# An MLP's second product with the activations held and 512 weight columns moved

## The chip, the cores and the metric

The kernel runs on one core of a Trainium2 chip. The time is that of the device for one execution, in microseconds (us); the median of three runs before the change is 1832.56 us (1829.42 to 1836.35).

## The reference

Two blocks in a row work on 256 tokens of 1024 channels, each with two layers. The change lies in the first block. After its attention mixers (four kinds, joined by w_out) each layer has an MLP:

```
for l in range(DEPTH):
    mod = c_act @ w_ada[l] + b_ada[l]
    sh1, sc1, g1, sh2, sc2, g2 = split(mod, 6)
    h = rmsnorm(x, norm_mix_g[l]) * (1 + sc1) + sh1
    x = x + g1 * (mixers(h @ w_in[l]) @ w_out[l])
    h = rmsnorm(x, norm_mlp_g[l]) * (1 + sc2) + sh2
    x = x + g2 * (square(relu(h @ w_up[l])) @ w_down[l])
return rmsnorm(x, final_norm_g)
```

w_up is 1024 x 4096, w_down 4096 x 1024, all in float32. The second block (a state-space scan, two attentions, gates) is the same before and after.

## The kernel before, in words

Activations lie with channels on the partitions and tokens along the free axis: x is 8 chunks of 128 channels by 256 tokens. Every large product is made of three float32r products: weight and activation are each split into a high part and the remainder (wh, wl; ah, al; uh, ul), and high x high, high x low and low x high are summed in PSUM. Weights stream from memory in tiles of 128 x 1024 (512 KB, here called half matrices) into eight buffers `w`. ScalarE copies a tile into `wh` (line 299), VectorE subtracts into `wl` (line 301); there are four buffers of each. `next_w` (line 304) asks for loads and splits ahead of their use.

The work is a queue of pieces (`add`, `fill`, `need`, lines 324 to 334). In the MLP, group g of 16 makes 256 of the 4096 hidden channels: `gemm` (line 339) runs 48 matmuls of the first product into a PSUM bank `g`, `ev_up` (line 1019) squares the positive part and splits it into uh and ul, tiles of the names pt0 and pt1. A group later `down` (line 1031) adds the second product of these 256 channels to four PSUM banks `acc` that stay for the whole MLP. In `down` the 128 x 128 weight block is held in the array and 256 tokens of uh or ul are moved past it; the result has channels on the partitions, as x has, and line 1085 adds it to x, bank by bank: two updates per bank, 128 x 256 each. The last group (`down_last`, line 1056) goes bank by bank, so that the updates of a finished bank run while the next is summed.

After layer 0 the statistics of x (`rms_wide`, line 454: squares, additions `fold`, a product `st` with ones, a power on GpSimd, a product `bc` that spreads the result) and eight half matrices each of two parts of the modulation (`ada_step`, line 551) come before the normalised chunks `ah` and `al` (`norm_apply`, line 599) and the first projections with w_in. After layer 1 the last product with the memory tokens (`tok_gemm`, line 383: it holds activations and moves 512 weight columns) runs on TensorE while the statistics are made, then the second block begins with `dt_gemm` (line 1265).

Which instruction stands where on each engine's queue is decided when the program is built, by a scheduler that simulates the engines; only the order is written into the program. Engines then run their queues strictly in order and wait on semaphores.

Of the kernel before, what the change touches and what calls it, by code (L numbers as in the profile page):

```python
# [13 lines left out]
ALU = mybir.AluOpType  # L14
PSUM = bass.MemoryType.PSUM

P = 128
S = 256
D = 1024
KC = D // P  # L20
# [473 lines left out]
def block1(e, ctx, mem0):  # L494
    nc, tc, d = e.nc, e.tc, e.d
    pool = lambda name: ctx.enter_context(tc.tile_pool(name=name, bufs=1))
    cp, zp, ap_ = pool("c1"), pool("z1"), pool("a1")
# [94 lines left out]
    def ada_add(tag, keys):  # L592
        for key in keys:
            e.add(tag, lambda key=key: (ada_pool if tag == "mlp" else ada_step)(*key[1:]))
# [26 lines left out]
    x = v3(e.unit("x"), KC)  # L621
# [368 lines left out]
    for l in range(DEPTH):  # L990
        mod = mods[l]
# [24 lines left out]
        acc = [e.bank("acc") for _ in range(4)]  # L1016
        us = {}

# [11 lines left out]

        def down(g):

            uh, ul = us[g]
            ws = {}

            def part(c, ms):
                if c not in ws:
                    ws[c] = e.next_w("w_down", l, g)
                wh, wl = ws[c]
                for m in ms:  # L1040
                    o = acc[m // 2][:, (m % 2) * S : (m % 2 + 1) * S]
                    sl = slice(m * P, (m + 1) * P)
                    fi = g == 0 and c == 0 and m % 2 == 0
                    la = g == 15 and c == 1
                    e.mm(o, wh[:, sl], uh[:, c, :], fi, False)
                    e.mm(o, wh[:, sl], ul[:, c, :], False, False)
                    e.mm(o, wl[:, sl], uh[:, c, :], False, la and m % 2 == 1)

            return part

        def down_piece(g, c):
            if c == 0:
                parts[g] = down(g)
            parts[g](c, range(KC))

        def down_last(g):
            part = down(g)
            for m in range(0, KC, 2):
                for c in range(2):
                    part(c, (m, m + 1))  # L1060

# [3 lines left out]

        parts, box, last = {}, [], {}
        steps = mlp_keys(l)
# [15 lines left out]
        ada_add("next", ad_next(l))  # L1083
        for k in range(KC):
            nc.vector.scalar_tensor_tensor(x[:, k, :], acc[k // 2][:, (k % 2) * S : (k % 2 + 1) * S], mod[:, 40 + k : 41 + k], x[:, k, :], ALU.mult, ALU.add)

# [641 lines left out]
```

## Time and profile before

| | before |
|---|---|
| median of 3 runs | 1832.56 us (1829.42 to 1836.35) |
| the profiled execution, its time | 1832.16 us |
| its span, first to last instruction | 1830.3 us |
| mean granted clock of TensorE (1 is 2.4 GHz, 0.5 is 1.2 GHz) | 0.991 |
| busy, of the span: TensorE matmuls | 98% |
| VectorE, ScalarE, GpSimd | 73%, 56%, 20% |
| chain that ended last: TensorE, VectorE, DMA, ScalarE | 89%, 4%, 3%, 3% |
| read from memory | 339 MB, 186 GB/s over the span |

Names in the profile are the program's without numbers: `acc<-pt,wh` is a matmul that writes acc and reads pt and wh. PE is TensorE, PEld its weight load, DVE is VectorE, ACT ScalarE, POOL GpSimd, SP the queue that issues the loads. A matmul's duration reaches from its start to the end of its result, and matmuls overlap; what a run of them costs is read from the start of one to the start of the next. The MLP of layer 0 lies at 216 to 404 us, that of layer 1 at 557 to 744 us.

### The profile page before, as it was taken

How to read it: one execution, taken by the hardware profiler on the slowest of the kernel's cores; microseconds unless marked ns; L12 is line 12 of the kernel's file. 1: busy time of each engine (PE TensorE's matmuls, PEld its weight loads, DVE VectorE, ACT ScalarE, POOL GpSimd, SP SyncE). 2: the span in 40 equal slices, each digit the busy share in tenths (PEclk: the TensorE clock that was granted, in tenths of full speed). 3: DMA queues.
4: the chain of work that ended last, by engine and by line, in shares of the span. 5: the costliest groups of instructions: out<-in, count | busy, mean ns of one | idle time of the engine just before them, and what ended most of it. 6: DMA issues, size and time to landing. Idle time of an engine off the chain costs nothing.

```text
span 1830.3 us, 36255 instructions
## 1 busy us (share of the span) xinstructions
PE 1789.1 (98%) x14344; PEld 1674.3 (91%) x14344; DVE 1333.6 (73%) x2209; ACT 1016.8 (56%) x1882; POOL 359.1 (20%) x291
## 2 busy tenths in 40 slices
PE   7999999999998999999999999999999999999998
PEld 6778799987888999998999999999999999999997
DVE  4575775756778655798897997576788797997566
ACT  4444444434555444567777575454556777675552
POOL 0000281800007200002444202200001444202200
PEclk9999999999998999999999999999999999999999
DMA  9873876758348655553444644465554445544451
GB/s 335 308 249 138 310 259 199 256 197 306 115 140 299 226 183 185 165 175 121 162 162 151 202 155 144 168 208 173 194 176 133 148 160 162 184 164 165 154 181 67
DMA packets 98219, 346.82 MB, mean 189 GB/s; under 512 B 12288, under 2 KB 13440, under 8 KB 97792
## 3 DMA queue, kind: packets, MB, share of 16 engines
q1 hardware_dynamic: 98048, 344.50, 55.5%
q8 instruction: 112, 1.84, 0.4%
q14 instruction: 59, 0.48, 0.1%
HBM read 339.01 MB, written 1.05 MB: 186 GB/s over the span
## 4 chain that ended last, share of the span: by engine, by line
PE 89%; DVE 4%; DMA 3%; ACT 3%; issue 1%; SPq 0%; POOLq 0%; DVEq 0%; POOL 0%; ACTq 0%
PE g L337 67%; PE acc L337 10%; PE yps L337 2%; DVE wl L301 1%; ACT wh L299 1%; PE ada L337 1%; PE o L337 1%; PE ds L337 1%; PE sc L337 1%; DMA w<-w_in 1%; PE do L337 1%; DMA w<-w_ada 1%; ACT sb L683 1%; PE xo L337 1%; DMA w<-w_up 1%
## 5 line engine op out<-in xcount | busy, mean ns | idle before, releaser
L301 DVE TENSOR_TENSOR wl<-w,wh 128x1024 fp32r<-128x1024 f32 x518 | 660.8, 1279 | 342.8 <-ACT wh L299 341.1
L299 ACT CAST wh<-w 128x1024 fp32r<-128x1024 f32 x518 | 540.5, 1047 | 494.9 <-PE g L337 328.8
L337 PE MATMUL g<-xh,wh 128*128 128x256 f32 x1664 | 478.2, 288 | 0.3
L337 PE MATMUL g<-xl,wh 128*128 128x256 f32 x1664 | 472.6, 284 | 0.0
L337 PE MATMUL g<-xh,wl 128*128 128x256 f32 x1664 | 471.8, 284 | 0.0
L337 PEld LDWEIGHTS g<-xh,wh 128*128 128x128 f32 x1664 | 319.8, 192 | 12.6 <-issue 6.2
L337 PEld LDWEIGHTS g<-xl,wh 128*128 128x128 f32 x1664 | 319.8, 192 | 0.9 <-issue 0.7
L337 PEld LDWEIGHTS g<-xh,wl 128*128 128x128 f32 x1664 | 319.9, 192 | 0.0
L337 PE MATMUL g<-ah,wh 128*128 128x256 f32 x736 | 211.5, 289 | 5.9 <-ACT ah L604 5.4
L337 PE MATMUL g<-ah,wl 128*128 128x256 f32 x736 | 210.6, 287 | 0.5 <-DVE wl L301 0.5
L337 PE MATMUL g<-al,wh 128*128 128x256 f32 x736 | 210.5, 287 | 0.5 <-DVE al L605 0.5
L403 POOL TENSOR_TENSOR rsy<-rv,mhalf 128x2 f32<-128x2 f32 (+1 forms) x14 | 14.5, 1038 | 936.8 <-DVE rv L420 830.1
L337 PE MATMUL acc<-pt,wh 128*128 128x256 f32 x1024 | 182.9, 280 | 0.0
L1505 POOL PARTITION_BROADCAST E<-rows x64 | 98.0, 1592 | 386.7 <-PE tw L1209 190.9
L1504 ACT ACTIVATE E<-E,ltok 128x128 f32<-128x128 f32 x384 | 124.3, 394 | 60.2 <-POOL E L1505 56.8
L337 PEld LDWEIGHTS acc<-pt,wh 128*128 128x128 f32 x1024 | 156.8, 188 | 0.5 <-issue 0.4
L337 PEld LDWEIGHTS g<-ah,wh 128*128 128x128 f32 x736 | 142.7, 195 | 9.8 <-ACT ah L604 6.4
L337 PEld LDWEIGHTS g<-al,wh 128*128 128x128 f32 x736 | 142.8, 194 | 2.7 <-DVE al L605 1.4
L337 PEld LDWEIGHTS g<-ah,wl 128*128 128x128 f32 x736 | 142.8, 194 | 1.2 <-DVE wl L301 0.7
L337 PE MATMUL acc<-pt,wl 128*128 128x256 f32 x512 | 142.3, 279 | 0.0
L583 POOL TENSOR_SCALAR sb<-w,ca 128x1024 f32<-128x1024 f32 x24 | 90.0, 3751 | 59.9 <-PE ada L337 32.8
L337 PEld LDWEIGHTS acc<-pt,wl 128*128 128x128 f32 x512 | 96.2, 188 | 0.0
(384 smaller groups left out, 3404.8 us busy)
## 6 DMA issues: line engine op xcount, KB each, us to landing
w<-w_ada SPq DMA_DIRECT2D x96, 512.0 KB
w<-w_up SPq DMA_DIRECT2D x64, 512.0 KB
w<-w_down SPq DMA_DIRECT2D x64, 512.0 KB
w<-w_br SPq DMA_DIRECT2D x64, 512.0 KB
w<-w_gl SPq DMA_DIRECT2D x48, 512.0 KB
w<-w_in SPq DMA_DIRECT2D x36, 512.0 KB
w<-w_xs SPq DMA_DIRECT2D x32, 512.0 KB
w<-w_z SPq DMA_DIRECT2D x32, 512.0 KB
```

Of the source, the lines that this page charges most:

```text
L299: nc.scalar.copy(wh, w)
L301: nc.vector.tensor_tensor(wl, w, wh.bitcast(F32), ALU.subtract)
L337: self.last_mm = self.nc.tensor.matmul(o, l, r, start=start, stop=stop)
L403: self.nc.gpsimd.tensor_tensor(y, v, self.mhalf[:, 0:cols], ALU.pow)
L583: nc.gpsimd.tensor_scalar(dst, w, ca[:, 2 * n + i : 2 * n + i + 1], None, ALU.mult)
L683: nc.scalar.activation(self.src(i), self.src(i), AF.Exp, bias=nmx[:, i : i + 1], scale=scale, accum_out=den[:, i : i + 1])
L1504: ex = lambda o, s, r: nc.scalar.activation(o, o, AF.Exp, bias=bias[:, s, r : r + 1])
L1505: nc.gpsimd.partition_broadcast(E, state["rows"][32 * (h % 4) : 32 * (h % 4) + 1, :])
```

## The change

In `down` the roles are exchanged: a 128 x 128 block of the activations is held (128 hidden channels by 128 tokens) and 512 columns of the weights are moved. A triple of matmuls now fills one bank, acc[2n + t], for 512 output channels (n) and 128 tokens (t), so that there are half as many matmuls with twice the columns. The result has tokens on the partitions; for x it has to be turned. After the last group each bank is copied into SBUF (`ys`; ScalarE for t = 0, VectorE for t = 1, in buffers of the names pt0 and pt1), `down_turn` transposes it in blocks of 128 x 128 on TensorE into a bank `at` (16 transposes per layer), and the 8 updates of x read `at`. The turn of the first 512 channels is queued after the third bank, the other at the end. The updates move from behind the queue's end into `down_turn`.

```diff
--- before.py
+++ after.py
@@ -1014,7 +1014,7 @@
         nc.vector.scalar_tensor_tensor(A2, mod[:, 32:40], 1.0, g_mlp[:, l * KC : (l + 1) * KC], ALU.add, ALU.mult)
         norm_apply(x, bc0, A2, mod[:, 24:32], ah, al)
         acc = [e.bank("acc") for _ in range(4)]
-        us = {}
+        us, wd, ys = {}, {}, {}
 
         def ev_up(g):
             def ev(ps):
@@ -1028,42 +1028,50 @@
                 us[g] = (v3(uh, 2), v3(ul, 2))
             return ev
 
-        def down(g):
+        def down(g, t, n, c):
 
             uh, ul = us[g]
-            ws = {}
-
-            def part(c, ms):
-                if c not in ws:
-                    ws[c] = e.next_w("w_down", l, g)
-                wh, wl = ws[c]
-                for m in ms:
-                    o = acc[m // 2][:, (m % 2) * S : (m % 2 + 1) * S]
-                    sl = slice(m * P, (m + 1) * P)
-                    fi = g == 0 and c == 0 and m % 2 == 0
-                    la = g == 15 and c == 1
-                    e.mm(o, wh[:, sl], uh[:, c, :], fi, False)
-                    e.mm(o, wh[:, sl], ul[:, c, :], False, False)
-                    e.mm(o, wl[:, sl], uh[:, c, :], False, la and m % 2 == 1)
-
-            return part
+            if (g, c) not in wd:
+                wd[g, c] = e.next_w("w_down", l, g)
+            wh, wl = (w[:, n * 512 : (n + 1) * 512] for w in wd[g, c])
+            o, ts = acc[2 * n + t], slice(t * P, (t + 1) * P)
+            e.mm(o, uh[:, c, ts], wh, g == 0 and c == 0, False)
+            e.mm(o, uh[:, c, ts], wl, False, False)
+            e.mm(o, ul[:, c, ts], wh, False, g == 15 and c == 1)
 
         def down_piece(g, c):
-            if c == 0:
-                parts[g] = down(g)
-            parts[g](c, range(KC))
+            for n in range(2):
+                for t in range(2):
+                    down(g, t, n, c)
+
+        def down_turn(n):
+
+            for p in range(2):
+                tps = e.bank("at")
+                for i in range(2):
+                    for t in range(2):
+                        nc.tensor.transpose(tps[:, i * S + t * P : i * S + (t + 1) * P], ys[n, t][:, (2 * p + i) * P : (2 * p + i + 1) * P], e.ident)
+                for i in range(2):
+                    k = 4 * n + 2 * p + i
+                    nc.vector.scalar_tensor_tensor(x[:, k, :], tps[:, i * S : (i + 1) * S], mod[:, 40 + k : 41 + k], x[:, k, :], ALU.mult, ALU.add)
 
         def down_last(g):
-            part = down(g)
-            for m in range(0, KC, 2):
-                for c in range(2):
-                    part(c, (m, m + 1))
+
+            for n in range(2):
+                for t in range(2):
+                    for c in range(2):
+                        down(g, t, n, c)
+                    ys[n, t] = e.t(ap_, [P, 512], "pt1", bufs=2) if t else e.t(ap_, [P, 1024], "pt0", bufs=2)[:, 0:512]
+                    (nc.vector.tensor_copy if t else nc.scalar.copy)(ys[n, t], acc[2 * n + t])
+                    if (n, t) == (1, 0):
+                        down_turn(0)
+            down_turn(1)
 
         def late_mem():
             with tc.issue_after(last["dve"].ins), tc.issue_after(last["act"].ins):
                 box.append(load_mem(e))
 
-        parts, box, last = {}, [], {}
+        box, last = [], {}
         steps = mlp_keys(l)
         for g in range(17):
             if l + 1 == DEPTH and g == 1:
@@ -1081,8 +1089,6 @@
                     e.add("mlp", lambda p=p: ada_rows(*p))
         e.need("mlp")
         ada_add("next", ad_next(l))
-        for k in range(KC):
-            nc.vector.scalar_tensor_tensor(x[:, k, :], acc[k // 2][:, (k % 2) * S : (k % 2 + 1) * S], mod[:, 40 + k : 41 + k], x[:, k, :], ALU.mult, ALU.add)
 
     for k in range(MEM, 6):
         mem_gemm(e, 0, k, box[0], mk0, mv0)
```

The rows below are the built programs' queues, out<-moving operand, held operand for matmuls. First TensorE in the loop of layer 0, where a piece of the first product (g) ends and one of the second (acc) begins, before:

```order
L337 MATMUL g_2588<-ah_2263,wh_2515 128x256
L337 MATMUL g_2588<-al_2264,wh_2515 128x256
L337 MATMUL g_2588<-ah_2263,wl_2517 128x256
L337 MATMUL acc_2381<-pt_449_2511,wh_2545 128x256 x2
L337 MATMUL acc_2381<-pt_449_2511,wl_2547 128x256
```

and now:

```order
L337 MATMUL g_2564<-ah_2263,wh_2515 128x256
L337 MATMUL g_2564<-al_2264,wh_2515 128x256
L337 MATMUL g_2564<-ah_2263,wl_2517 128x256
L337 MATMUL acc_2381<-wh_2533,pt_449_2511 128x512
L337 MATMUL acc_2381<-wl_2535,pt_449_2511 128x512
```

The moved operand was pt (the activations) and is now wh or wl; x2 marks two alike in a row, the products with uh and ul, which lie in one tile; now they come from the held operand, and the one with ul comes third. One half matrix feeds 12 matmuls where it fed 24.

At the end of layer 0, VectorE's queue in the normalisation (nt and al are its two steps for a chunk, wl the split of a half matrix of w_in, mod a part of the modulation), before:

```order
L572 TENSOR_TENSOR mod_14_106<-adat_4591,pack_1_70 128x2x4
L605 SCALAR_TENSOR_TENSOR al_4518<-nt_4662,mod_14_106,ah_4517 128x256
L605 SCALAR_TENSOR_TENSOR al_4518<-nt_4666,mod_14_106,ah_4517 128x256
L603 SCALAR_TENSOR_TENSOR nt_4670<-x_386,A_707_4515,bc_4539 128x256
L603 SCALAR_TENSOR_TENSOR nt_4674<-x_386,A_707_4515,bc_4539 128x256
L605 SCALAR_TENSOR_TENSOR al_4518<-nt_4670,mod_14_106,ah_4517 128x256
L605 SCALAR_TENSOR_TENSOR al_4518<-nt_4674,mod_14_106,ah_4517 128x256
L603 SCALAR_TENSOR_TENSOR nt_4678<-x_386,A_707_4515,bc_4539 128x256
L603 SCALAR_TENSOR_TENSOR nt_4682<-x_386,A_707_4515,bc_4539 128x256
L605 SCALAR_TENSOR_TENSOR al_4518<-nt_4678,mod_14_106,ah_4517 128x256
L605 SCALAR_TENSOR_TENSOR al_4518<-nt_4682,mod_14_106,ah_4517 128x256
L603 SCALAR_TENSOR_TENSOR nt_4686<-x_386,A_707_4515,bc_4539 128x256
```

and now:

```order
L605 SCALAR_TENSOR_TENSOR al_4162<-nt_4314,mod_14_106,ah_4161 128x256
L605 SCALAR_TENSOR_TENSOR al_4162<-nt_4318,mod_14_106,ah_4161 128x256
L572 TENSOR_TENSOR mod_14_106<-adat_4302,pack_1_70 128x2x4
L603 SCALAR_TENSOR_TENSOR nt_4322<-x_386,A_715_4159,bc_4183 128x256
L301 TENSOR_TENSOR wl_4252<-w_4248,wh_4250 128x1024
L603 SCALAR_TENSOR_TENSOR nt_4326<-x_386,A_715_4159,bc_4183 128x256
L605 SCALAR_TENSOR_TENSOR al_4162<-nt_4322,mod_14_106,ah_4161 128x256
L603 SCALAR_TENSOR_TENSOR nt_4330<-x_386,A_715_4159,bc_4183 128x256
L605 SCALAR_TENSOR_TENSOR al_4162<-nt_4326,mod_14_106,ah_4161 128x256
L603 SCALAR_TENSOR_TENSOR nt_4334<-x_386,A_715_4159,bc_4183 128x256
L301 TENSOR_TENSOR wl_4386<-w_4258,wh_4384 128x1024
L605 SCALAR_TENSOR_TENSOR al_4162<-nt_4330,mod_14_106,ah_4161 128x256
```

Splits now stand between the chunks; four in all come before the last al, where before the first one came behind all eight chunks. On TensorE at the same place (g with one number is one projection), before:

```order
L337 MATMUL g_4713<-al_4518,wh_4423 128x256
L337 MATMUL g_4713<-ah_4517,wl_4425 128x256
L337 MATMUL g_4713<-ah_4517,wh_4453 128x256
L337 MATMUL ada_4595<-w_4583,ca_11_101 32x256 x4
L337 MATMUL g_4713<-al_4518,wh_4453 128x256
L337 MATMUL g_4713<-ah_4517,wl_4455 128x256
```

and now:

```order
L337 MATMUL g_4357<-ah_4161,wl_4077 128x256
L337 MATMUL adat_4302<-pack_1_70,pt_752_4300 128x4 x2
L337 MATMUL g_4415<-ah_4161,wh_4244 128x256
L337 MATMUL g_4415<-al_4162,wh_4244 128x256
L337 MATMUL g_4357<-ah_4161,wh_4075 128x256
L337 MATMUL g_4415<-ah_4161,wl_4246 128x256
```

Before, matmuls of the first projection alternate with half matrices of the modulation (ada). Now all of these stand before it but for the turn of the last one (adat), and the first projection alternates with the second, and further on with the third. The statistics st stand behind 13 half matrices, where they stood behind 9; the 16 transposes lie among the second to fifth.

At the end of layer 1, VectorE's queue, before:

```order
L1085 SCALAR_TENSOR_TENSOR x_386<-acc_6266,mod_14_106,x_386 128x256 x2
L1085 SCALAR_TENSOR_TENSOR x_386<-acc_6267,mod_14_106,x_386 128x256 x2
L1085 SCALAR_TENSOR_TENSOR x_386<-acc_6268,mod_14_106,x_386 128x256 x2
L438 TENSOR_TENSOR fold_8355<-pt_1287_8351,pt_1288_8353 128x512
L1085 SCALAR_TENSOR_TENSOR x_386<-acc_6269,mod_14_106,x_386 128x256 x2
L301 TENSOR_TENSOR wl_8299<-w_8078,wh_8297 128x1024
L1120 CAST identr_8470<-pack_1_70 128x128
L1125 MEMSET one_8475 64x128
L301 TENSOR_TENSOR wl_8376<-w_8114,wh_8374 128x1024
```

and now:

```order
L1065 COPY pt_1296_7593<-acc_5911 128x512
L1065 COPY pt_1300_7623<-acc_5913 128x512
L301 TENSOR_TENSOR wl_7580<-w_7410,wh_7578 128x1024
L301 TENSOR_TENSOR wl_7664<-w_7446,wh_7662 128x1024
L301 TENSOR_TENSOR wl_7776<-w_7772,wh_7774 128x1024
L1056 SCALAR_TENSOR_TENSOR x_386<-at_7603,mod_14_106,x_386 128x256 x2
L1056 SCALAR_TENSOR_TENSOR x_386<-at_7610,mod_14_106,x_386 128x256 x2
L1056 SCALAR_TENSOR_TENSOR x_386<-at_7625,mod_14_106,x_386 128x256 x2
L1056 SCALAR_TENSOR_TENSOR x_386<-at_7632,mod_14_106,x_386 128x256 x2
L438 TENSOR_TENSOR fold_7643<-pt_1303_7639,pt_1304_7641 128x512
```

The updates of x read acc and came first; now two copies and three splits stand before them, and they read the transposed banks. On TensorE the 16 transposes stand between the 46 matmuls that precede the statistics there. The scheduler's order differs in the mixers of layer 1 and in a few places behind as well.

## Rows read from the trace of the kernel before

**Rows 1.** The page of the kernel before: engines' busy time, costliest groups.

```profile
PE 1789.1 (98%) x14344; PEld 1674.3 (91%) x14344; DVE 1333.6 (73%) x2209; ACT 1016.8 (56%) x1882; POOL 359.1 (20%) x291
...
L301 DVE TENSOR_TENSOR wl<-w,wh 128x1024 fp32r<-128x1024 f32 x518 | 660.8, 1279 | 342.8 <-ACT wh L299 341.1
L299 ACT CAST wh<-w 128x1024 fp32r<-128x1024 f32 x518 | 540.5, 1047 | 494.9 <-PE g L337 328.8
```

**Rows 2.** Chain of waits in order of time: start us, us, what.

```profile
252.40 5.66 PE acc L337 x48
...
739.00 4.99 PE acc L337 x44
743.99 10.47 PE g L337 x46
759.32 2.56 PE g L337 x12
767.17 36.60 PE g L337 x305
```

**Rows 3.** The same chain, asked for 430 to 575 us.

```profile
489.60 0.87 PE tp L708 x8
```

**Rows 4.** Groups by shape, TensorE: line, operation, xcount, busy us, mean ns, idle.

```profile
L337 PE MATMUL acc<-pt,wh 128*128 128x256 f32 x1024 | 182.9, 280 | 0.0
...
L708 PE MATMUL tp<-pack,sb 128*128 128x128 f32 x120 | 17.5, 278 | 1.9 <-DVE sb L695 1.8
```

**Rows 5.** What touches the tile acc: xcount, ns minimum/median/maximum, first and last start.

```profile
L1085 DVE SCALAR_TENSOR_TENSOR x<-acc,mod,x x16: 474/477/484, 400.0 to 744.6; 128x256 f32<-128x256 f32 x16
```

**Rows 6.** Timeline, TensorE, end of layer 0: start us, us, engine, operation, [idle before].

```profile
403.78 3.65 PE L337 MATMUL ada<-w,ca 128*32 128x256 f32 x62
408.69 0.64 PE L337 MATMUL ada<-w,ca 128*32 128x256 f32 x8 [1.26 <-DMA w<-w_ada]
409.26 0.61 PE L337 MATMUL st<-ones,fold 128*128 128x1 f32 x4
...
424.28 0.38 PE L337 MATMUL g<-ah,wl 128*128 128x256 f32 x1 [0.45 <-DVE wl L301]
```

**Rows 7.** Timeline, issuing queue, the same stretch.

```profile
404.46 4.02 SPq L289 DMA_DIRECT2D w<-w_ada  x8
```

**Rows 8.** Timeline, VectorE, the same stretch.

```profile
411.74 0.87 DVE L603 SCALAR_TENSOR_TENSOR nt<-x,A,bc 128x256 f32<-128x256 f32 x2 [1.61 <-PE bc L337]
...
418.36 0.89 DVE L605 SCALAR_TENSOR_TENSOR al<-nt,mod,ah 128x256 fp32r<-128x256 f32 x2 [0.19 <-ACT ah L604]
```

**Rows 9.** Timeline, TensorE, end of layer 1.

```profile
754.29 0.50 PE L337 MATMUL st<-ones,fold 128*128 128x1 f32 x4
755.84 0.71 PE L337 MATMUL bc<-pack,rsy 128*128 128x128 f32 x4 [1.05 <-POOL rsy L403]
757.67 0.58 PE L337 MATMUL dt<-xh,wh 128*128 128x256 f32 x1 [1.12 <-ACT xh L464]
```

**Rows 10.** Timeline, VectorE, end of layer 1.

```profile
744.17 0.87 DVE L1085 SCALAR_TENSOR_TENSOR x<-acc,mod,x 128x256 f32<-128x256 f32 x2
...
751.42 0.41 DVE L444 TENSOR_TENSOR fold<-fold 128x256 f32<-128x256 f32 x1
```

**Rows 11.** Stretches: us, busy us of each engine, granted clock, DMA share, GB/s.

```profile
403.85:424.30 20.45, 17.38 (x193) 11.37 (x193) 11.02 (x26) 7.92 (x15) 0.72 (x1) 1.00 0.93 349
424.30:438.00 13.70, 13.70 (x113) 13.55 (x114) 7.49 (x13) 5.15 (x9) 1.04 (x2) 1.00 0.92 360
480.00:510.00 30.00, 27.88 (x220) 23.70 (x217) 22.37 (x83) 15.15 (x42) 0.00 (x0) 0.94 0.26 84
510.00:540.00 30.00, 28.17 (x229) 24.22 (x228) 19.61 (x60) 15.82 (x41) 0.00 (x0) 1.00 0.37 120
540.00:574.70 34.70, 29.62 (x255) 27.69 (x254) 28.65 (x44) 17.87 (x27) 15.79 (x7) 0.85 0.77 281
...
757.67:770.00 12.33, 12.33 (x80) 12.33 (x81) 7.22 (x16) 5.85 (x13) 0.00 (x0) 0.75 0.16 48
```

## The prediction

> **What bounds the kernel now.** Three views, in this order. The page first: TensorE is busy for 1789.1 of 1830.3 us, VectorE for 1333.6 [rows 1]; the reader is to see that hardly any place is left in which TensorE is idle, so that a gain must be TensorE time or a wait of TensorE. Then the chain of waits in order of time [rows 2]: the loop over the MLP's groups is an unbroken run of pieces of 48 matmuls, the second product's at 5.66 us each, with no wait between. VectorE and ScalarE split the streamed weights there at 1.28 and 1.05 us per half matrix [rows 1] and are ahead. Last the timelines of the two ends of that loop [rows 6 to 10], where TensorE does wait: after layer 0 for the weights of the modulation and for the normalisation, after layer 1 for the norm's statistics. The loop decides what the change gains, the two ends what of it is kept.
>
> **The loop.** Removed: 2 x 768 matmuls that move 256 columns. A piece of 48 takes 5.66 us, 117.9 ns each [rows 2]; the 276 to 280 ns that the grouped rows give is one matmul from start to end, of which most lies over its neighbours [rows 4]. Added: 2 x 384 that move 512 columns. TensorE runs just such a stream right after layer 1's MLP, 46 in 10.47 us, 227.6 ns each, with weights in the same form [rows 2]. Two old ones cost 235.8 ns, so each pair saves 8.2 ns: 768 x 8.2 = 6.3 us. The last 44 of layer 1 run at 113.4 ns already (4.99 us) [rows 2], which takes 0.2 back: 3.15 us in layer 0, 2.95 in layer 1, 6.1 in all. Bounds: nothing (the loop stays at 117.9 ns per 256 columns), and 768 x 22.5 = 17.3 us if 512 columns went at one per cycle of 2.4 GHz (213.3 ns). I take the row, which is the same shape at the same clock. The low part of the split weights is now needed by the second matmul of a triple, not the third; it is finished a piece ahead, so this costs nothing.
>
> The Trainium skill (TensorE: Matmul & The Clock Gate, Back-to-back issue gap) gives a sustained spacing of about 131 ns for matmuls of 512 columns. The row here shows 227.6 ns; by the page 768 x (235.8 - 131) = 80 us would go, and that is a rival below with the little chance that the row leaves it.
>
> **The transposes.** Added: 32, 16 behind each layer's last group. Eight in a row took 0.87 us, 109 ns each [rows 3]; 32 x 0.109 = 3.5 us, 1.75 per layer. Bounds: nothing, where TensorE would wait anyway, and 32 x 0.278 = 8.9 us if each ran its whole duration alone [rows 4]. I take 109 ns, since they stand in runs of up to 8.
>
> The skill speaks against the change here (the same page, Part 4: PE-mode transpose): in a kernel about 275 ns for one of 128x128. The mean of one agrees, 278 ns, but the spacing of the run is 109; by the page's figure the sum would be 5.3 us worse.
>
> **The results' way back.** Four copies out of PSUM per layer are new, two on VectorE and two on ScalarE; the 8 updates of x stay, at 477 ns [rows 5], and read the transposed bank. Before, each pair of updates followed its bank during the last group, and only one pair came after the last matmul; now all 8 come after it.
>
> **End of layer 0.** The last matmul of the MLP comes 3.15 us earlier, at T' = 400.7 instead of 403.8 [rows 6]. What follows are 16 half matrices of modulation weights, eight of them in the buffers, the other eight asked for as those come free: the ninth is asked for at 404.46 [rows 7] and used at 408.69 [rows 6], 4.2 us later. In the new order the first half matrix is used before the last group, so the loads are one ahead: the tenth now lands at T' + 4.8, six more follow at 1.5 us (0.52 MB at the 349 GB/s of that stretch [rows 11]), the sixteenth lands at 414.5. The transposes and 1.75 us of TensorE lie under this. The statistics (st) moved from behind the ninth to behind the thirteenth: T' + 4.8 + 3 x 1.5 + 0.6 = 410.6, against 409.26 [rows 6]. From st to the first normalised chunk 2.5 us, to the last 10 [rows 6, 8]. VectorE's queue now has four weight splits between the chunks; they cost 4 x 1.28 and about 1 us of waiting for the first of these weights: last chunk at 426.5 instead of 419.3. That would be a loss, but TensorE's order changed with it: the first three projections (144 matmuls at 120 ns [rows 2], 17.3 us) run chunk by chunk, interleaved, where before the first ran alone against the chunks until 424 and the other two came after it. They start at 415.1 and end at 432.4 if TensorE never waits, I take 433.3; before they ended at 438.0 [rows 11], of which 1.65 us were statistics that now come later. So TensorE is 436.3 - 433.3 = 3.0 us ahead there, transposes paid. Bounds: 4 ahead (no wait), 3 behind (if the splits' wait for weights stretches to the end).
>
> **End of layer 1.** TensorE has 46 matmuls of another product (10.5 us) to do before the statistics, which start at 754.29, and the sums they need are ready at 751.83: 2.5 us of slack [rows 2, 9, 10]. Now 16 transposes stand among the 46, st could start 12.2 us after the last matmul instead of 10.5. But VectorE's queue has one copy (0.7) and three splits (3.7, the third held up to T' + 3.7 by its ScalarE half) ahead of the 8 updates (3.5): x is ready at T' + 8.4, where before it was at T + 1.2 (745.04) [rows 10]. From there one square, three additions, two splits and small work: 6 us, T' + 14.4. The slack is gone and 2.2 us more. Then st to the first dt matmul: 3.4 us before [rows 9], with one split beside it; now that split stands ahead of the statistics' own VectorE step, 4.0. Sum T' + 18.4 against T + 13.9: +4.5, less the 2.95 of the loop: 1.5 us later. Bounds: 1.2 earlier (slack holds), 3 later.
>
> **Elsewhere.** The scheduler also reorders layer 1's mixers. The work is the same; what can change is TensorE's idle time, 2.1 + 1.8 + 5.1 = 9 us between 480 and 574.7 [rows 11]. I take 0, bounds 4.5 either way.
>
> **Sum.** -3.0 + 1.5 + 0 = -1.5 us on the profiled execution's 1832.16 (span 1830.3 and 1.86 around it), which is 0.4 below the median 1832.56: 1831.0.
>
> **Rivals.**
> - The ends keep everything: slack in layer 1 holds (-1.2), layer 0 gives 3.0, and the reordered mixers halve their idle time (-4.5): -8.7, 1823.9. For it: the waits there are short and for different engines. Against: VectorE's queue behind layer 1. Chance 0.20.
> - Slower: TensorE is fed one chunk at a time for 11 us after layer 0, and the granted clock falls to its 1.2 GHz level. After layer 1 it did so after waits of 1.05 and 1.12 us [rows 9]: 213 ns per matmul for 6 us, then 120 [rows 2], 0.75 in that stretch, and 0.85 over 540 to 574.7, where 5.2 us were lost [rows 11]. With the 3.0 lost, 5.2 for the clock, 1.5 for layer 1 and 4.5 in the mixers: +11.2, 1843.8. It decides from a wait for the splits' weights about as long as the 5.1 us idle of that stretch; against it, 403.85 to 424.3 has 3.1 us of idle at full clock [rows 11]. Chance 0.12.
> - The 512-column stream is no faster in the loop, where VectorE, ScalarE and GpSimd are all at work: +6.1 on the forecast, 1837.1. Against: the measured stream ran beside busy engines too. Chance 0.13.
> - 131 ns per matmul: 80 us less, about 1753. The row speaks against it. Chance 0.01.
>
> **How the numbers follow.** The forecast has 0.54, from 1826.5 to 1836 by the bounds above that don't add up. 0.5% (9.2 us) is about what a measurement of this kernel tells from no change: faster means below 1823.4, slower above 1841.7. The first rival spreads from 1820 to 1828, a third of it is faster, with the last rival and a little for ends that both gain 0.10. The slower rival is mostly over the line, 0.09, and 0.01 from the third. The rest, 0.80, is the same. The range goes from 1822 to 1841.
>
> **What would show it.** Right: pieces of 24 matmuls at 5.46 us in the loop; runs of 8 transposes under 1 us; st after layer 1 waiting for VectorE's sum; projections of layer 1 ending about 3 us sooner. Wrong: pieces at 5.66 us; a clock under 1.00 between 400 and 440; TensorE idle in layer 1's mixers by more than 13 us or less than 5; a transpose that waits for a copy.

## The result, and the profile after

The changed kernel takes 1845.25 us (1843.29 to 1848.05), the kernel before beside it 1833.82: ratio 1.0066, interval 1.0041 to 1.0091. It is slower by 10 to 12 us; the prediction said 1831.0, from 1822 to 1841. Run again beside other kernels it took 1842.85 against 1832.65 (1.0056, 1.0042 to 1.0070). The first profiled execution after, which is read here, took 1848.05, with a span of 1846.3.

The page after, with the lines that answer to [rows 1, 4]; TensorE's busy time is 6.6 us longer, VectorE's split takes 19 ns more:

```profile
PE 1795.7 (97%) x13608; PEld 1642.9 (89%) x13608; DVE 1341.8 (73%) x2213; ACT 1018.6 (55%) x1886; POOL 362.5 (20%) x291
...
L301 DVE TENSOR_TENSOR wl<-w,wh 128x1024 fp32r<-128x1024 f32 x518 | 670.2, 1298 | 330.7 <-ACT wh L299 328.9
...
L337 PE MATMUL acc<-wh,pt 128*128 128x512 f32 x512 | 166.2, 396 | 0.0
```

Where the time went is read from the starts of a few instructions that both kernels have, in the timelines of TensorE. Each number is the us from one of them to the next, "again" is the second profile of the changed kernel:

| stage | before | after | again |
|---|---|---|---|
| start to the first acc matmul of layer 0 | 229.66 | 232.59 | 227.68 |
| acc loop of layer 0, to the end of the last acc matmul | 174.12 | 172.96 | 172.97 |
| from there to the statistics st before layer 1's MLP | 146.05 | 152.54 | 151.79 |
| to the first acc matmul of layer 1 | 21.64 | 23.69 | 24.22 |
| acc loop of layer 1 | 172.36 | 171.50 | 171.37 |
| from there to the first dt matmul | 13.84 | 17.43 | 17.94 |
| the rest | 1072.63 | 1075.59 | 1072.43 |

The first and the last row hold the same work in both kernels; they are 5.9 us longer in one profile and 2.2 shorter in the other, so that is taken as no effect of the change (over all profiles of this case the first row goes from 227.4 to 232.6, the last from 1071.5 to 1077.4). The rows between sum to +10.1 and +10.3 us: 2.0 and 2.1 won in the loops, 6.5 and 5.7 lost behind layer 0, 2.1 and 2.6 before layer 1's MLP, 3.6 and 4.1 behind layer 1.

The loop, in the chain of waits in order of time, as [rows 2]: a piece now takes 5.60 us for 24 matmuls, 233.3 ns each, where 5.46 was forecast; the two merged lines at the end show the same, 7.47 / 32.

```profile
255.17 5.60 PE acc L337 x24
...
741.78 7.47 PE acc L337 x32
...
749.71 3.73 PE acc L337 x16
```

The end of layer 0, TensorE's timeline, as [rows 6]:

```profile
405.55 1.06 PE L337 MATMUL ada<-w,ca 128*32 128x256 f32 x14
406.55 0.44 PE L1053 MATMUL at<-pack,pt 128*128 128x128 f32 x2
406.92 0.62 PE L337 MATMUL ada<-w,ca 128*32 128x256 f32 x4
407.47 0.87 PE L1053 MATMUL at<-pack,pt 128*128 128x128 f32 x6
408.28 0.64 PE L337 MATMUL ada<-w,ca 128*32 128x256 f32 x8
408.85 1.09 PE L1053 MATMUL at<-pack,pt 128*128 128x128 f32 x8
409.87 3.22 PE L337 MATMUL ada<-w,ca 128*32 128x256 f32 x54
414.61 0.64 PE L337 MATMUL ada<-w,ca 128*32 128x256 f32 x8 [1.52 <-DMA w<-w_ada]
417.24 0.64 PE L337 MATMUL ada<-w,ca 128*32 128x256 f32 x8 [1.99 <-DMA w<-w_ada]
417.81 0.75 PE L337 MATMUL st<-ones,fold 128*128 128x1 f32 x4
...
419.68 1.23 PE L337 MATMUL bc<-pack,rsy 128*128 128x128 f32 x4
...
423.35 0.58 PE L337 MATMUL g<-ah,wh 128*128 128x256 f32 x1
```

The last acc matmul gives way at 405.55. The 16 transposes, in three places, take 2.2 us from start to start (0.37 + 0.81 + 1.02). Then TensorE waits for the 12th and the 13th half matrix, and only behind them comes st, 12.3 us after the MLP, where before it came at 5.5. VectorE had the sum by 414.5. The first projection starts at 17.8 us, before at 9.8. The same stretches by the table of stretches (columns as in [rows 11]):

```profile
405.55:409.87 4.32, 4.32 (x44) 2.40 (x43) 2.51 (x6) 1.22 (x2) 0.00 (x0) 1.00 0.57 187
409.87:417.81 7.94, 4.43 (x72) 1.96 (x71) 3.82 (x8) 2.15 (x4) 0.00 (x0) 1.00 0.91 282
417.81:423.35 5.54, 5.43 (x41) 3.25 (x37) 2.46 (x8) 0.91 (x2) 0.72 (x1) 0.53 1.02 416
423.35:434.00 10.65, 10.65 (x87) 10.65 (x84) 9.18 (x16) 6.89 (x11) 0.00 (x0) 0.92 1.03 405
```

The loads moved at 187 and 282 GB/s where 349 was counted on. Behind the two waits the granted clock goes to its 1.2 GHz level (0.53 over the 5.5 us), and nearly everything between st and the first projection runs at half speed. Four such bc matmuls took 0.71 us at the end of layer 1 [rows 9], here 1.23. The lower level lasts for 6.8 us here (from 418.13) and for 10.2 in the second profile, in which it takes in the first 4.4 us of the projections.

The end of layer 1, TensorE, as [rows 9], and VectorE's stretch before it:

```profile
766.45 0.61 PE L337 MATMUL st<-ones,fold 128*128 128x1 f32 x4 [0.72 <-DVE fold L444]
768.99 0.71 PE L337 MATMUL bc<-pack,rsy 128*128 128x128 f32 x4 [1.94 <-POOL rsy L403]
770.71 0.58 PE L337 MATMUL dt<-xh,wh 128*128 128x256 f32 x1 [1.01 <-ACT xh L464]
```

```profile
753.45:766.40 12.95, 12.28 (x62) 9.90 (x61) 12.49 (x25) 8.61 (x13) 0.00 (x0) 1.00 0.56 179
```

From the end of the last acc matmul (753.45) to st VectorE is busy for 12.49 of 12.95 us, and TensorE's own 62 instructions take 12.28. Both are late now; before, TensorE's 46 took 10.3 and VectorE was done 2.5 us ahead of them [rows 9, 10].

### The profile page after: what moved, and what is told of

It is laid out like the page before. It is cut to its first block, busy times and chain, and to the rows that moved or that the text cites. A ratio compares the mean times of both kernels' runs of the same rounds, so it can differ in the third digit from the quotient of the medians.

```text
span 1846.3 us, 34796 instructions
## 1 busy us (share of the span) xinstructions
PE 1795.7 (97%) x13608; PEld 1642.9 (89%) x13608; DVE 1341.8 (73%) x2213; ACT 1018.6 (55%) x1886; POOL 362.5 (20%) x291
## 3 DMA queue, kind: packets, MB, share of 16 engines
q8 instruction: 107, 1.75, 0.4%
HBM read 339.01 MB, written 1.05 MB: 184 GB/s over the span
## 4 chain that ended last, share of the span: by engine, by line
PE 90%; DVE 3%; ACT 3%; DMA 2%; issue 1%; POOL 0%; POOLq 0%; SPq 0%; DVEq 0%; ACTq 0%
PE g L337 67%; PE acc L337 10%; PE yps L337 1%; PE ada L337 1%; DVE wl L301 1%; PE o L337 1%; PE sc L337 1%; ACT wh L299 1%; PE ds L337 1%; PE do L337 1%; PE xs L337 1%; PE xo L337 1%; DMA w<-w_up 1%; DMA w<-w_in 1%; ACT sb L683 1%
## 5 line engine op out<-in xcount | busy, mean ns | idle before, releaser
L301 DVE TENSOR_TENSOR wl<-w,wh 128x1024 fp32r<-128x1024 f32 x518 | 670.2, 1298 | 330.7 <-ACT wh L299 328.9
L337 PE MATMUL acc<-wh,pt 128*128 128x512 f32 x512 | 166.2, 396 | 0.0
L337 PEld LDWEIGHTS g<-ah,wh 128*128 128x128 f32 x736 | 142.9, 195 | 13.0 <-ACT ah L604 7.7
L337 PEld LDWEIGHTS acc<-wh,pt 128*128 128x128 f32 x512 | 96.2, 188 | 22.2 <-issue 0.4
L337 PE MATMUL acc<-wl,pt 128*128 128x512 f32 x256 | 101.3, 396 | 0.0
L1292 DVE SCALAR_TENSOR_TENSOR cv<-g,pack,cv 128x254 f32<-128x254 f32 (+1 forms) x192 | 89.3, 476 | 2.3 <-ACT cv L1289 0.4
```

Source lines behind the costliest of these rows:

```text
L301: nc.vector.tensor_tensor(wl, w, wh.bitcast(F32), ALU.subtract)
L337: self.last_mm = self.nc.tensor.matmul(o, l, r, start=start, stop=stop)
L1292: nc.vector.scalar_tensor_tensor(a_[:, a:b], p_[:, a + j - 2 : b + j - 2], conv_w[:, i0 + j : i0 + j + 1], a_[:, a:b], ALU.mult, ALU.add)
```

## The experiments

Each is timed against the kernel before on the same chip. "st +x" is the start of the statistics, x us after the MLP's last matmul.

**e1 and e2: one layer each.** The MLP's second product is chosen by layer:

```diff
+        if l == 0:
+            def down(g, t, n, c):
...
+        else:
+            parts = {}
+            def down(g):
...
+        if l != 0:
+            for k in range(KC):
+                nc.vector.scalar_tensor_tensor(x[:, k, :], acc[k // 2][:, (k % 2) * S : (k % 2 + 1) * S], ...)
```

(in e2 with 1 for 0).

> Only layer 0's MLP has the new product with its transposes; layer 1 is as before. Theory A (the loss of 11.4 us lies at the ends of the two MLPs, where the turned result makes the norm's statistics late, and most of it after layer 0, where the statistics now stand behind 13 half matrices of the modulation, wait for their loads and start after 3.5 us of idle TensorE): the end of layer 0 looks as in the changed kernel, statistics 12 us after the last matmul of the MLP, clock about 0.5 in the 5 us behind them; 5 to 8 us slower than before. Theory B (the transposes and copies themselves are what costs, the same in either layer): half of 11.4, 5.7 us, but with the statistics less than 8 us behind the last matmul. Theory C (most of it is in the second block, off the change): under 3 us slower.

> Only layer 1's MLP has the new product; layer 0 and the mixers are as before. A: loop 1.3 us faster, first dt matmul 17.3 us after the MLP's last matmul instead of 13.7, so 2 to 3.5 us slower in all; with e1 the two add up to the 11.4 of the whole change within 3 us. B: 5.7 us slower. C: under 2 us, and the two don't add up.

e1: 1841.11 against 1834.21, ratio 1.0035 (1.0022 to 1.0048); e2: 1839.26, 1.0024 (1.0014 to 1.0035). They sum to 0.59%, the whole change has 0.66 and 0.56, so the two layers add up, and nothing is left for the second block (theory C falls). In e1 st comes at +11.4 and the clock is 0.64 behind it; in e2 dt at +17.4, as in the changed kernel. The medians lie 6.9 and 5.05 us above before, and for e2 theory A had 2 to 3.5: in its profile 3.6 us are lost at the end of layer 1, but 1.7 also behind layer 0, where nothing was changed, and the loop of layer 1 won only 0.1. Equal halves (B) would fit the two times as well, though not e1's late st: the next two decide.

**e3: no way back.** The copies and transposes are left out, and x takes the banks as they lie:

```diff
...
-                    (nc.vector.tensor_copy if t else nc.scalar.copy)(ys[n, t], acc[2 * n + t])
-                    if (n, t) == (1, 0):
-                        down_turn(0)
-            down_turn(1)
...
+        for k in range(KC):
+            nc.vector.scalar_tensor_tensor(x[:, k, :], acc[k // 2][:, (k % 2) * S : (k % 2 + 1) * S], ...)
```

> The new product in both layers, without the copies and the transposes: x takes the banks as they are, so it is not the reference's x. The scheduler then puts the statistics behind 9 half matrices again. A: only the loop is left, pieces of 24 at 5.60 us against 5.66, two loops 1.3 us faster each: 2 to 3 us faster than before, 1829 to 1833. If instead the held activations cost something in the loop that the pieces don't show: 5 us slower or more. If 512 columns ran at 227.6 ns once the turn is gone: 6 us faster.

1832.22 against 1834.21, 0.9991 (0.9980 to 1.0002): an interval that takes in no change, with a median 2.0 us below before. In its profile the two loops are 2.1 us shorter, as in the changed kernel, and st is at +5.9, behind 10 half matrices. But the stage behind layer 0 is 3.2 us shorter than before and the last row of the table 4.2 longer, so the time alone doesn't show it; the loops' 2 us are what the 512 columns are worth, before their way back is paid.

```profile
239.90 5.60 PE acc L337 x24
```

**e4: the late statistics alone.** The kernel before, product and all, with st placed behind 13 half matrices:

```diff
+            e.fill(13)
+            e.st_after = e.last_mm.ins
             bc0 = norm_stats(x)
...
+        with self.tc.issue_after(self.st_after) if ...:
             self.token_sum(st, a, P, True, True)
```

> The kernel before, with nothing changed in the product, but the statistics after layer 0 placed behind 13 half matrices of the modulation, as the changed kernel has them (the scheduler then also interleaves the first projections and puts four splits between the normalised chunks, as there). A: statistics 11 to 12.5 us behind the last matmul instead of 5.5, clock under 0.7 for about 5 us, 4 to 6 us slower than before without one transpose. B: no change, within 2 us, since the projections that are interleaved make up for the late start.

1842.07 against 1834.21, 1.0040 (1.0028 to 1.0052): more than was expected, without one transpose. TensorE's timeline and the stretch behind it:

```profile
411.45 0.64 PE L339 MATMUL ada<-w,ca 128*32 128x256 f32 x8 [1.44 <-DMA w<-w_ada]
...
415.31 1.02 PE L339 MATMUL st<-ones,fold 128*128 128x1 f32 x4
```

```profile
415.30:420.50 5.20, 5.08 (x37) 2.68 (x33) 1.76 (x5) 0.91 (x2) 0.72 (x1) 0.50 1.03 415
```

Waits for the loads of the same half matrices (1.04 us for the 9th, 1.44, 0.59 and 0.54 for the 11th to 13th), the same half clock; the stage to the statistics before layer 1's MLP takes 152.16 us, as long as after (146.05 before).

**e5: st earlier, nothing else.** The changed kernel, with the half matrices from the 12th on queued behind st:

```diff
+            if l == 1 and tag_next and nhalf[0] >= 11:
+                with tc.issue_after(e.st_mm.ins):
+                    blocks(boxes[l, s], ca32[:, 2 * n + i, :], w, ...)
```

> The changed kernel with the statistics after layer 0 behind 11 half matrices of the modulation instead of 13; the rest of the order stays within a few instructions. Theory A (e4: the place of the statistics behind loads that are still on their way is the cost there): x is summed 9 us after the MLP's last matmul, so the statistics start at 9 to 9.5 us instead of 12.3, the first projection 3 us sooner, and the whole 2.5 to 4 us below the changed kernel, 7 to 9 us above before. Theory D (it is the four splits between the chunks and the interleaved projections that cost, whatever the statistics do): within 1 us of the changed kernel, 11 us above before.

1843.1 against 1835.12, 1.0054 (1.0041 to 1.0067). By the ratio that is little or nothing below the changed kernel; the medians are 8.0 us apart, which the first theory had, but the stage behind layer 0 takes 151.74 us as in the changed kernel. st came as expected, but three half matrices now stood between it and bc, where the changed kernel has one:

```profile
410.28 0.61 PE L337 MATMUL st<-ones,fold 128*128 128x1 f32 x4 [1.49 <-DVE fold L444]
...
415.11 1.22 PE L337 MATMUL bc<-pack,rsy 128*128 128x128 f32 x4
```

401.26 is the MLP's end here: st at +9.0, bc at +13.9 and the first projection at +17.5, as late as in the changed kernel: st alone, moved forward, brought nothing forward behind it.

**e6: splits behind the updates after layer 1.**

```diff
     bc = norm_stats(x)
+    e.split_after = last["x"].ins
     e.need("mem")
+    e.split_after = None
...
+            with self.tc.issue_after(self.split_after) if ...:
                 nc.vector.tensor_tensor(wl, w, wh.bitcast(F32), ALU.subtract)
```

> The changed kernel with the splits for the last memory product queued behind the updates of x on VectorE after layer 1: one split stands before the updates instead of three. If VectorE's queue is what makes the statistics late there (13.2 us behind the last matmul instead of 10.5): statistics at 10.7 to 11.5, dt at 15 to 15.5 instead of 17.4, 2 us below the changed kernel. If the copies and transposes themselves bound it: no change. If the split weights come too late for TensorE: idle time among the 46 memory matmuls, and no gain.

1847.55, 1.0079 (1.0064 to 1.0093): wrong in every theory. The splits went from before the updates to before the additions, six in all ahead of the sum where there were five, and st came at +16.5 in this profile:

```profile
767.10 0.61 PE L340 MATMUL st<-ones,fold 128*128 128x1 f32 x4 [4.05 <-DVE fold L447]
```

**e7: e4 with TensorE kept busy.** Before the 9th, 11th, 12th and 13th half matrix stand 8, 12, 6 and 8 matmuls of the identity by itself:

```diff
...
+            dum = e.bank("dum")
+            for j in range(FILL[k]):
+                with tc.issue_after(e.last_mm.ins):
+                    e.mm(dum[:, 0:P], e.ident, e.ident, True, True)
```

> As e4 (the kernel before with late statistics), but with 34 matmuls of constants (128 columns, into a bank that nobody reads) placed in the waits for the 9th, 11th, 12th and 13th half matrix, so that TensorE isn't idle there; the projections' order behind changes with it. If the idle time lowers the clock: granted clock 1.00 from 415 to 420 us where e4 had 0.50, and 2 to 4 us below e4, 4 us above before. If the clock falls for another reason or doesn't matter there since the loads bound it: within 1 us of e4.

1845.09, 1.0053 (1.0041 to 1.0066), no better than e4. The clock did what was expected:

```profile
403.80:416.00 12.20, 11.71 (x144) 8.75 (x136) 2.96 (x6) 2.68 (x5) 0.00 (x0) 1.00 0.90 324
416.00:421.00 5.00, 5.00 (x62) 3.46 (x55) 0.81 (x2) 1.50 (x2) 0.72 (x1) 1.00 1.03 415
```

1.00 where e4 had 0.50. But each filler is two matmuls in the trace and took 239 ns (12 from 410.69 to 413.56), which put st to +15.7, and the scheduler ordered the projections otherwise. So with the waits filled the clock stayed up; it fell later, for 3.4 us from 424.62, behind a wait of 1.31 us for the first chunk. What the clock alone costs, this run doesn't say.

**e8: the order in a triple.** The product with the low activation second, as before:

```diff
-            e.mm(o, uh[:, c, ts], wl, False, False)
-            e.mm(o, ul[:, c, ts], wh, False, g == 15 and c == 1)
+            e.mm(o, ul[:, c, ts], wh, False, False)
+            e.mm(o, uh[:, c, ts], wl, False, g == 15 and c == 1)
```

> The changed kernel with the three products in the order of before: high x high, low activation x high weight, high activation x low weight, so that the same weights are moved twice in a row and the held block changes with every matmul. If the order in a triple sets the spacing: pieces of 24 at 5.46 us (227.6 ns) or lower instead of 5.60, 3 us below the changed kernel. If not: 5.60 us, and within 2 us of the changed kernel.

1848.49, 1.0076 (1.0064 to 1.0088), 2 to 4 us above the changed kernel by the ratios, most of it in the stage behind layer 0 (155.40 us). The pieces stay at 5.60 us:

```profile
241.48 5.60 PE acc L337 x24
```

**e9, e10 and e11: ways to make up for it.** e9: the second block's splits behind the last addition (fold, line 444). e10: e9, and after layer 0 the half matrices from the 10th on queued behind st, from the 11th on behind bc (the diff stands at e13). e11: e10, and the last bank's matmuls queued behind the first half's transposes:

```diff
     e.need("mem")
+    e.split_after = e.fold_ins.ins
...
-                    for c in range(2):
-                        down(g, t, n, c)
+                    with tc.issue_after(last["turn"].ins) if n and t else contextlib.nullcontext():
+                        for c in range(2):
+                            down(g, t, n, c)
```

> The changed kernel with the weight splits of the second block queued behind the last addition of the sums after layer 1 on VectorE (in e6 they stood behind the updates but ahead of the additions). Theory: VectorE's queue of 5 splits among copies, updates and additions is what makes the statistics late there. Then statistics 10.5 to 11 us behind the last matmul instead of 13.2, dt at 14 to 15 instead of 17.4, 2 to 3 us below the changed kernel. Rival: the transposes stand late in TensorE's queue and bound it, 12.5 us and less than 1 us gained.

> As e9, and after layer 0 the statistics behind 9 half matrices and the product bc that spreads them behind 10, as in the kernel before. In e5 the statistics came 3 us sooner but bc still stood behind the 13th half matrix, and nothing was gained. If that order is what costs: statistics at 9 us (when x is summed), bc at 11, first projection at 14 to 15 us instead of 17.8, 4 to 6 us below the changed kernel with e9's gain, 1840. If the wait of 3 us for the sums lowers the clock just as the wait for loads did: clock near 0.5 for 3 to 5 us in that stretch and 2 us less of a gain, 1842.

> As e10, and the first half of the result is turned before the last bank of the last group, so that half of x's updates run beside the last matmuls, as all but two did in the kernel before. x summed about 6 us behind the last matmul instead of 9, first projection at 11 to 12, end of layer 0 within 3 us of before, statistics after layer 1 at 10.5; 6 to 10 us below the changed kernel, 1835 to 1839. If the transposes and the copy of the last bank bound it: no better than e10.

e9: 1845.16 against 1832.65, 1.0066 (1.0053 to 1.0080). The sums were ready 11.8 us after the MLP (the last addition ends at 760.50, the MLP at 748.72), still later than expected, and st came at +12.3 without a wait: the rival was right, the transposes in front of it on TensorE bound it there, though VectorE is only 0.5 us ahead. Then three splits stood before VectorE's own step of the norm, and bc waited for that:

```profile
761.01 0.50 PE L340 MATMUL st<-ones,fold 128*128 128x1 f32 x4
765.74 1.22 PE L340 MATMUL bc<-pack,rsy 128*128 128x128 f32 x4 [4.23 <-POOL rsy L406]
```

e10: 1843.31, 1.0061 (1.0048 to 1.0073); the stage behind layer 0 fell to 147.47 us, dt stayed late (+19.4). Against e9 the 5 us that this stage gained in the profile are only 1.8 us between the medians (0.05% between the ratios); the last row of the stage table is 1077.35 us long in this profile, 1075.41 in e9. e11: 1851.02, 1.0100 (1.0087 to 1.0114), wrong outright: the last bank, held back behind the transposes, is summed later, and the loops take 3.9 and 4.6 us longer than in e10. The copy, updates, squares and additions of the last bank still follow it, so that the statistics of layer 0 come 3.3 us later than in e10, counted from the first acc matmul (185.3 against 182.0), and TensorE waits 4.8 us for them.

```profile
413.95 0.99 PE L340 MATMUL st<-ones,fold 128*128 128x1 f32 x4 [4.76 <-DVE fold L447]
```

**e12: the changed kernel again.**

> The changed kernel itself beside the others, for another profile: 9 to 13 us above before; statistics 11.5 to 12.5 us behind the last matmul of layer 0, the clock near 0.5 behind them, statistics 13.2 us behind that of layer 1; and the first 230 us and the second block, which the change doesn't touch, should not repeat the 2.9 and 3.0 us that they were longer in the first profile.

1842.85 against 1832.65, as expected, and the first and the last row of the table are not longer here. st at +11.5 (+13.2 in layer 1), and behind the first

```profile
412.19:418.00 5.81, 5.73 (x41) 3.52 (x37) 2.45 (x8) 0.91 (x2) 0.72 (x1) 0.50 1.01 391
```

**e13 and e14: the order of before, alone.** e13 is e10 without e9's moved splits; e14 the same with the new product in layer 0 only:

```diff
-            blocks(boxes[l, s], ca32[:, 2 * n + i, :], e.next_w("w_ada", l, s, n), ...)
+            w = e.next_w("w_ada", l, s, n)
+            if l == 1 and tag_next and nhalf[0] >= 9:
+                with tc.issue_after((e.bc_mm if nhalf[0] >= 10 else e.st_mm).ins):
+                    blocks(boxes[l, s], ca32[:, 2 * n + i, :], w, ...)
+            else:
...
```

nhalf counts the half matrices of that modulation.

> The changed kernel with nothing else changed than the order after layer 0: the statistics behind 9 half matrices and bc behind 10, as before (e10 without the moved splits). If the place of the statistics and of bc costs what e4 added to the kernel before: 3.5 to 5 us below the changed kernel, 1838 to 1840, first projection at 16 us, layer 1's statistics reached 4 to 5 us sooner. If what e10 gained there was only the clock of that profile: within 1.5 us of the changed kernel, 1842 to 1845.

> The same order of before after layer 0, with the new product in layer 0 only (e1 with the statistics behind 9). If the order costs 4 us of e1's 6.9: 2 to 4 us slower than before, 1836 to 1838. If not: as e1, 1841.

e13: 1840.87 against 1833.86, 1.0035 (1.0022 to 1.0048), where the changed kernel has 1.0066 and 1.0056. e14: 1836.15, 1.0012 (1.0000 to 1.0024), where e1 has 1.0035. Both gain 0.2 to 0.3%, some 4 to 5 us. In e13 TensorE waits for the sums, then st and bc follow with one half matrix between, and six half matrices come behind, so that the first projection, expected at +16, still starts at +16.9:

```profile
409.35 1.01 PE L337 MATMUL st<-ones,fold 128*128 128x1 f32 x4 [2.35 <-DVE fold L444]
410.30 1.08 PE L337 MATMUL ada<-w,ca 128*32 128x256 f32 x8
411.49 1.22 PE L337 MATMUL bc<-pack,rsy 128*128 128x128 f32 x4
```

(400.33 is the end of the MLP.) The stage takes 147.29 us in e13 and 147.98 in e14. Over all profiles it takes 142.9 to 148.5 us where bc stands behind 10 or 11 half matrices, and 150.6 to 155.4 where it stands behind 14 or more. The order that the scheduler took is thus what most of the loss behind layer 0 is. It is the place of the statistics that was moved: e13 still has three splits between the chunks and interleaved projections, against theory D of e5. The clock falls in e13 too (0.59 from st to the first projection). Where the 4.5 us between e12 and e13 lie is read by adding up, for each operation, the time from its start to the next one's:

| stage behind layer 0, us | before | after | e12 | e13 |
|---|---|---|---|---|
| ada, with its waits | 14.0 | 16.7 | 16.0 | 15.6 |
| transposes at | - | 2.2 | 2.2 | 2.2 |
| st, bc, adat | 4.0 | 5.0 | 5.6 | 5.3 |
| projections and products g | 80.2 | 79.1 | 80.0 | 78.1 |
| attention sc, o | 24.2 | 25.4 | 23.8 | 21.6 |
| all else | 23.7 | 24.1 | 24.2 | 24.5 |

Less than 1 us of the 4.5 lies at st, bc and ada themselves; the rest is in the projections and attentions that follow, which the scheduler orders otherwise when the statistics move. By the end of the first three projections (their 144 matmuls end at +36.1, in e12 at +37.3, and e13 has 0.9 us more of other work ahead of that) some 2 us of the 4.5 are won, the others in the mixers behind. Which of these moves gives it, no run tells apart. No version that gives the reference's x beat the kernel before.

## Why the prediction was wrong

Of the 11.6 us between the forecast (-1.5) and the rows that the change touches (+10.1), 4.1 lie in the loops, 6.3 behind layer 0 and 2.1 before layer 1's MLP; the end of layer 1 gives 0.9 back.

**The loop: wrong, by a term that was sized from two different places.** 6.1 us were forecast, 2.0 measured. The old piece was read in the loop (117.9 ns per matmul), the new one from the 46 behind layer 1 (227.6). But the chain shows the old matmuls at 113.4 ns in the 5 us ahead of those 46 [rows 2]: there 2 x 113.4 = 226.8 stands against 227.6, nothing won at all. Within the loop it is 2 x 117.9 = 235.8 against 233.3, so 768 x 2.5 = 1.9 us. The prediction named the 113.4 and used it for a correction of 0.2; it should have barred the comparison. The third rival (no faster in the loop) was nearly right on this.

The Trainium skill (TensorE: Matmul & The Clock Gate, Back-to-back issue gap) gives about 131 ns as the sustained spacing at 512 columns; 233.3 ns were measured, and the 80 us that would have followed are not there.

**The transposes: size about right, cover wrong.** 109 ns each was forecast, 137 measured in layer 0. Of the 1.75 us per layer the sum let the wait for loads hide those of layer 0. But the waits did not shrink by them: TensorE's idle time in the stage behind layer 0, added up over its stretches, was 7.0 us before, 7.7 after and 7.0 in the second profile.

**The end of layer 0: the step that failed.** The prediction had TensorE 3.0 us ahead at the end of the first projections, which beside the loop's 3.15 is 0.15 lost behind the MLP, and nothing for the mixers; 6.5 and 5.7 us were lost there. It had seen that st now stood behind the 13th half matrix, and put it 9.9 us after the MLP; it came at 12.3 and 11.5, since the 12th and 13th landed 9.1 and 11.7 us behind it in the first profile, not 7.8 and 9.3. It had the first projection at 14.4 (415.1 - 400.7); it came at 17.8 and 17.4. And it priced the stretch between the two at full clock, though its own rows showed the clock fall behind waits of 1.05 and 1.12 us at the end of layer 1. Then it let the interleaved projections make up for the late start, with the first three done at 32.6 (433.3 - 400.7). They did not: they were done at 36.4 and 37.3, and e4, which puts the old product into the same order, has 36.3. Before, they were done at 34.0 with the 1.65 us of statistics that now come later, so 4.0 and 4.9 us of the 6.5 and 5.7 were lost by then; the 2.5 and 0.9 that are left lie in the mixers, within the bounds given for them.

The rival with the falling clock, at 1843.8, comes nearest to what happened, but for the place: the clock fell behind waits between half matrices, ahead of the chunks and not among them. That its number came so near is in part luck: it has 4.5 us for the mixers, and nothing for the loop's missing 4.1 or for the stretch before layer 1's MLP. Its condition (a wait of about 5 us) does not hold either, and no length of a single wait tells the runs apart there: the clock fell behind waits of 1.52 and 1.99 us in the changed kernel, of 1.49 in e2, where this end is as before, and of three of 0.85 to 0.95 in e8; it stayed at 1.00 through 1.26 in the kernel before [rows 6] and through 1.67 and 0.88 in e3. In e2 the stage took 147.80 us. What decides, these runs don't show. One of the prediction's own signs of being wrong had named it: a clock under 1.00 between 400 and 440.

**Before layer 1's MLP: not priced.** Between st and the first projection there 2.0 us were lost in both profiles; the other 0.5 of the second lies behind that. The norm's step on VectorE stands behind a split that waits for a load of w_up, and then GpSimd's power meets the next split. Before, it started 0.14 us ahead of that split, after 0.16 us behind its start, and took longer, first before, then after:

```profile
553.25 0.70 POOL L403 TENSOR_TENSOR rsy<-rv,mhalf 128x2 f32<-128x2 f32 x1 [113.72 <-DVE rv L420]
```

```profile
562.63 1.62 POOL L403 TENSOR_TENSOR rsy<-rv,mhalf 128x2 f32<-128x2 f32 x1 [112.50 <-DVE rv L420]
```

**The end of layer 1: right.** 4.5 us were forecast from the last acc matmul to dt, 3.6 and 4.1 measured (17.43 and 17.94 against 13.84). st came at +13.2, not 14.4. The reason given, VectorE's queue, is a part of it: with three splits fewer ahead of the sum in e9, st still came at +12.3, behind the transposes on TensorE, where the prediction had 12.2 for TensorE alone.

## What to carry to other kernels

When a shape is replaced by another, take both spacings from the same stretch; a difference of 4% between two stretches was here larger than the difference between the shapes. When a result comes later by some us, look at what the built order now puts ahead of its first reader, up to the last link of the chain (here st and bc), and price the loads that these instructions wait for and the clock behind the wait; an added transpose cost less than the place to which it moved the statistics. Before such a change, run the new product without its way back: e3 would have shown that there were 2 us to win.

## What the runs showed of the hardware

At a granted clock of 1.00 throughout, matmuls of one shape ran at two spacings: 117.9 and 113.4 ns for 256 columns, 233.3 and 227 for 512. In the kernel before, the faster one began within a run of the same instructions, in the last group of layer 1 (at about 738.8 us), and lasted for 5 us in which VectorE and ScalarE were busy and idle by turns and the loads moved 205 GB/s on average; the order of a triple (e8) does not set it. What does stays open.

GpSimd's power of 128 x 2 elements took 1.61 to 1.84 us in every one of the 61 places, over all 16 profiles, where a split of VectorE was already running when it started, and ended 0.55 us or more behind that split. In the 131 other places it took 0.70 to 0.80 us, but for one of 2.37 in e11, also where a split began while it ran.
